# Input projection of an encoder layer: four 512-column chunks taken in two pairs of 1024 columns

## The chip, the cores and the metric

The kernel runs on one core of a Trainium2 chip. The metric is device time in microseconds (us) of one execution; of several executions the median is taken. The core has five engines with queues of their own, which run in parallel and wait for each other through semaphores: PE (TensorE, the matrix engine; PEld is its weight load), DVE (VectorE), ACT (ScalarE), POOL (GpSimd) and SP (SyncE, which here only issues DMAs). An instruction that waits holds up everything behind it in its engine's queue. Matrix products go to PSUM, 8 banks of 512 float32 columns on 128 partitions; all other on-chip data is in SBUF.

## The reference, cut to what matters

One encoder layer on 1024 positions of width 1024. The change touches the input projection and what directly uses its columns.

```python
D_MODEL = 1024; SEQ = 1024; HEAD_DIM = 64; N_HEADS_A = 8; N_KV_A = 2; N_HEADS_B = 8; D_FF = 2816
# w_in: (1024, 2304) -> [qA 512 | kA 128 | vA 128 | qB 512 | kB 512 | vB 512]
hn = rms_norm(x, norm1_g)
proj = hn @ w_in
qa = apply_axial_rope(rms_norm(qa, qa_norm_g), tables)
ka = apply_axial_rope(rms_norm(ka, ka_norm_g), tables)
out_a = global_gqa_attention(qa, ka, va)
out_b = dilated_mixture_attention(rms_norm(qb, qb_norm_g), rms_norm(kb, kb_norm_g), vb)
mixed = jnp.concatenate([rms_norm(out_a, outa_norm_g), rms_norm(out_b, outb_norm_g)], axis=-1)
x = x + mixed @ w_out
x = x + conv_ffn(rms_norm(x, norm2_g), w_up, conv_w, conv_b, w_down)
```

## The kernel before

**Arithmetic.** Everything is float32. An operand of a matrix product is split into a high part (`fp32r`, rounded) and a low part (the rest), and a product takes three matmuls: high by high, high by low, low by high. The split costs one ACT copy (the high part, `bigr<-bigf` in the profile) and one DVE subtraction (the low part, `bigr<-bigf,bigr`).

**Stages.** Load and transpose-load x; the input projection; mixer A (dense attention), mixer B (dilated attention), output projection, up-projection with convolution and gate, down-projection. The input projection has two parts. 256 columns (kA and vA) are done plainly, by `kv_proj(i)` for eight tiles of 128 positions, 24 matmuls of 128x256 each. The other 2048 columns are four chunks of 512, in the order kb, vb, qa, qb, and each chunk is one 2x2 Strassen step: seven products (numbers 1 to 7) of a 512x512 sum of x blocks (`a_op`) by a 512x256 sum of weight blocks. `in_product(m)` is one such product: four tiles of 128 positions, four slices of 128 of the inner dimension, three matmuls of 128x256, so 48 matmuls; there are 28 products.

**Around a product.** `w_load` fetches half a chunk of weights (1 MB), `w_scale` multiplies it by the norm gain on ACT (four instructions of 128x512), `w_prep(m)` forms the weight sum of product m on DVE and splits it (three buffers of 1024 high and 1024 low elements). `in_group(m)` says which two PSUM banks take the product, one of three pairs of banks. `in_out(m)` brings the product out: for numbers 1, 5, 2 and 7 an ACT copy of 128x1024, for 6, 3, 4 and 7 DVE sums; number 6 is added to three other sums in SBUF. `x_squares(i)` squares a tile of x in natural layout (for the norm), with the squares written to PSUM banks that nothing else needs there, and then fetches tile i+2 into the same one of two buffers. `kv_out(i)` copies a tile of kA and vA out of its bank (`kv_bank`, banks 2 to 5). `s_split` makes the x sums of products 3, 5, 6 and 7. `done` makes of a finished chunk what attention needs: squares, norm, rotary turn (on POOL), table products, or a DMA to DRAM. The K heads of mixer A go through `k_fetch`, `k_norm`, `k_turn` (POOL), `k_add`, `k_split` and `k_ready`, spread over products 11 to 27. What remains for qa and qb at the end of the phase is put in a list `late`, from which the attention stages take pieces.

**What sets the order.** All operations are recorded in the order of the Python code, and a list scheduler (`Recorder.simulate`) places them: it prices each operation, follows the dependences, keeps PE nearly in program order and lets other engines take what is ready by their priorities. The result is a fixed order of instructions on each engine. A change in one place therefore can reorder others. Every operation is emitted from one line, L442 before (L444 after), so the groups of a profile are told apart by engine, operands (`bigr` the split operands, `bigf` other SBUF data, `ps` PSUM) and shape.

Of the kernel before, what the change touches and what calls it, by code (L numbers as in the profile page):

```python
# [39 lines left out]
NF = O_F + 9232  # L40
# [20 lines left out]
F_UA = O_F + 1024  # L61
F_WA = (O_F + 2048, O_F + 4096)
F_WC = O_F + 6144
F_NAT = (O_F, O_F + 4096)
F_KVT = O_F + 5120
F_KSQ = O_F + 4096
F_ROPE = O_F + 8192
# [378 lines left out]
def tile_encoder_layer(ctx, tc, x, xt, w_kv, w_in, gains, outg, norm2_g, w_out, w_up, conv,  # L446
# [104 lines left out]
    chunks = ["kb", "vb", "qa", "qb"]  # L551
    prods = [(c, n) for c in range(4) for n in ((1, 5, 2, 7, 6, 3, 4) if c else (1, 2, 5, 7, 6, 3, 4))]
# [44 lines left out]
    def kv_bank(tt):  # L597
        return 2 + tt % 4
# [85 lines left out]
    def w_buf(c, half):  # L684
        return F_WC if half else F_WA[c % 2]

    def w_load(c, half):
        dma(f(w_buf(c, half), 2048), w_in[c, half])

    def w_scale(c, half):  # L690
        for k in range(4):
            o, g = f(w_buf(c, half) + 512 * k, 512), f(SM_G1 + 4 * half + k, 1)
            act(o, o, AF.Copy, scale=g)

    def w_op(m):
        return R_WR + 2048 * (m % 3)

    def w_prep(m):
        if m >= len(prods):
            return  # L700
        c, n = prods[m]
        b11, b12, b21, b22 = [fp(w_buf(c, half) + 256 * u, [512, 4], [1, 256]) for half in range(2) for u in range(2)]
        eng = vec
# [18 lines left out]

    def in_product(m):
        c, n = prods[m]
        w = w_op(m)
        for t in range(4):
            a = a_op(n, t)
            o = PS[:, in_group(m) + 256 * t:in_group(m) + 256 * t + 256]
            for k in range(4):
# [4 lines left out]
                mm(o, al, wh, start=False, stop=(k == 3), skip_group_check=True)

    def c_at(c, t0, u):

        return qab(t0 if c else 4 - t0) + 512 * (c % 2) + 256 * u

    def in_out(m):  # L740
        c, n = prods[m]
# [4 lines left out]
        if n == 1:
            act(ua, g, AF.Copy)
        elif n == 5:
            act(c12, g, AF.Copy)
        elif n == 2:  # L750
            act(c11, g, AF.Copy)
            if c:
                fin(0, 0)
        elif n == 7:
            act(c21, g, AF.Copy)
            add(vec, c22, g, c12)
        elif n == 6:
            add(vec, ua, g, ua)
            for o, eng in ((c22, vec), (c12, vec if c else gp), (c21, vec if c else gp)):
                if c == 3:  # L760

                    last_sums.append(lambda o=o: add(vec, o, o, ua))
                else:
                    add(eng, o, o, ua)
            if c == 0:
                fin(0, 0)
            fin(4, 1)
        elif n == 3:
            add(vec, c12, g, c12)
# [4 lines left out]

    later, deferred, going, n_done, last_sums = [], [], [], [0], []

    def done(c, t0, u, late=None):
# [4 lines left out]

        def v_out():
            for t in range(t0, t0 + 4):
                v = f(o + 1024 * (t - t0), 256)
                act(v, v, AF.Copy, scale=f(SM_R1 + t, 1))
                dma(rows(vscr, t), heads(v, 4))
# [996 lines left out]
```

## Time and profile before

| what | value |
|---|---|
| time, three runs | 1284.65, 1285.03 and 1285.33 us, median 1285.03 |
| the profiled execution, its own time | 1285.81 us |
| its span, first to last instruction | 1284.0 us |
| granted TensorE clock | 1.000 of full speed |
| DVE busy | 1084.5 us, 84% of the span |
| ACT busy | 741.0 us, 58% |
| POOL busy | 112.0 us, 9% |
| DMA moved | 156.99 MB, mean 122 GB/s |

The profiled execution's own time is 1.8 us longer than its span; that stretch lies around the first and last instruction. Busy times of a pipelined PE run from the start of one matmul to its modelled end, so neighbours overlap; rates are therefore read from counts in a window or from the length of an unbroken piece of the chain, not from the mean duration of one matmul. Windows of the span are given in us from the first instruction. The input projection lies between about 10 and 205 us.

### The profile page before, as it was taken

To read this page: it belongs to the slowest core of one execution; us is meant where nothing else is said; L and a number is where in the kernel's file an instruction comes from. 1 tells how busy PE (TensorE), PEld (TensorE's weight loads), DVE (VectorE), ACT (ScalarE), POOL (GpSimd) and SP (SyncE) were. 2 spreads that over 40 slices of the span, in tenths; PEclk is the share of its full clock that TensorE was granted. 3 is DMA by queue.
4 is the path that set the end of the run, shared out by engine and by line. 5 is a ranking of instruction groups with operands and counts; after the bars stand their busy time and mean duration, and the time that the engine had idled before them with its cause. 6 is when DMAs were issued, how large, how long until landed. Compare 5 with 4: busy or idle time off the path is not lost.

```text
span 1284.0 us, 19129 instructions
## 1 busy us (share of the span) xinstructions
PE 1269.3 (99%) x6916; PEld 1080.9 (84%) x6916; DVE 1084.5 (84%) x1906; ACT 741.0 (58%) x1192; POOL 112.0 (9%) x117
## 2 busy tenths in 40 slices
PE   7999999999999999999999999999999999999998
PEld 7999998878888888878888888888888888878887
DVE  6987789999988877897689999999999998776664
ACT  7865467998888776763455444444444444343331
POOL 0011053200212222000120000000000000000000
PEclk9999999999999999999999999999999999999999
DMA  8534211000004554343222322333322347977863
GB/s 334 178 74 116 83 39 55 10 9 1 1 9 113 131 143 101 109 158 131 74 89 68 123 91 75 115 107 107 123 92 83 106 160 259 314 260 234 284 220 113
DMA packets 118206, 156.99 MB, mean 122 GB/s; under 512 B 50656, under 2 KB 75744, under 8 KB 117088
## 3 DMA queue, kind: packets, MB, share of 16 engines
q1 hardware_dynamic: 116816, 152.36, 37.0%
q0 software_dynamic: 1152, 3.15, 0.9%
q8 instruction: 54, 0.88, 0.3%
q10 hardware_dynamic: 144, 0.27, 0.1%
q14 instruction: 40, 0.33, 0.1%
HBM read 117.73 MB, written 33.82 MB: 118 GB/s over the span
## 4 chain that ended last, share of the span: by engine, by line
PE 89%; DVE 4%; DMA 4%; ACT 1%; issue 1%; SPq 0%; ACTq 0%; DVEq 0%
PE ps L442 89%; DVE bigr L442 2%; DVE bigf L442 2%; DMA bigf<-rscr 1%; ACT bigr L442 1%; DMA bigf<-gscr 1%; DMA gscr<-bigf 0%; DMA bigf<-w_down 0%; DMA bigf<-w_out 0%; DMA bigf<-w_kv 0%; ACT L442 0%; SPq L442 0%; ACT bigf L442 0%; ACT ps L442 0%; ACTq L442 0%
## 5 line engine op out<-in xcount | busy, mean ns | idle before, releaser
L442 PE MATMUL ps<-bigr 128*128 128x512 f32 (+3 forms) x6532 | 1238.5, 349 | 9.1 <-ACT bigr L442 6.5
L442 PEld LDWEIGHTS ps<-bigr 128*128 128x128 f32 x6532 | 1042.7, 187 | 183.5 <-ACT bigr L442 13.2
L442 ACT ACTIVATE bigr<-bigf 128x512 fp32r<-128x512 f32 (+2 forms) x358 | 270.6, 770 | 302.4 <-PE ps L442 224.4
L442 DVE TENSOR_TENSOR bigr<-bigf,bigr 128x512 fp32r<-128x512 f32 (+2 forms) x326 | 280.7, 872 | 50.6 <-ACT bigr L442 46.8
L442 DVE TENSOR_TENSOR bigf<-bigf 128x512 f32<-128x512 f32 (+3 forms) x298 | 215.3, 746 | 29.4 <-DMA bigf<-w_down 22.4
L442 DVE TENSOR_TENSOR bigf<-ps,bigf 128x512 f32<-128x512 f32 (+3 forms) x262 | 177.8, 686 | 50.6 <-PE ps L442 43.2
L442 ACT ACTIVATE bigr<-ps 128x512 fp32r<-128x512 f32 (+1 forms) x292 | 167.7, 603 | 85.5 <-PE ps L442 83.3
L442 ACT ACTIVATE bigf<-bigf 128x1024 f32<-128x1024 f32 (+5 forms) x186 | 142.7, 794 | 65.8 <-DVE bigf L442 52.5
L442 DVE SCALAR_TENSOR_TENSOR bigf<-bigf 128x255 f32<-128x255 f32 (+5 forms) x283 | 162.5, 590 | 8.4 <-ACT bigf L442 4.9
L442 DVE TENSOR_TENSOR bigr<-ps,bigr 128x512 fp32r<-128x512 f32 x188 | 127.0, 684 | 29.6 <-ACT ps L442 20.5
L442 ACT ACTIVATE ps<-ps 128x512 f32<-128x512 f32 x192 | 115.3, 602 | 9.4 <-PE ps L442 8.5
L442 ACT ACTIVATE bigf<-ps 128x512 f32<-128x512 f32 (+3 forms) x112 | 71.2, 638 | 56.9 <-PE ps L442 39.7
L442 DVE TENSOR_REDUCE bigf<-ps 128x1 f32<-128x512 f32 x128 | 81.7, 680 | 1.9 <-PE ps L442 1.8
L442 POOL TENSOR_TENSOR bigf<-bigf 128x128 f32<-128x128 f32 (+3 forms) x54 | 56.5, 1071 | 236.3 <-DVE bigf L442 235.9
L442 POOL TENSOR_TENSOR bigr<-bigf,bigr 128x512 fp32r<-128x512 f32 x32 | 42.8, 1341 | 269.7 <-ACT bigr L442 189.3
L442 PE MATMUL ps<-bigf 128*128 128x128 f32 (+2 forms) x384 | 63.0, 294 | 1.4 <-DVE bigf L442 1.3
L442 PEld LDWEIGHTS ps<-bigf 128*128 128x128 f32 (+2 forms) x384 | 43.3, 140 | 15.1 <-DVE bigf L442 2.5
L442 DVE CUSTOM_DVE_ANT_1 bigf<-ps,bigf 128x432 bf16<-128x432 f32 x64 | 38.5, 602 | 2.9 <-PE ps L442 1.9
L442 DVE CUSTOM_DVE_ANT_0 bigf<-ps,bigf 128x256 bf16<-128x256 f32 x64 | 26.9, 420 | 2.5 <-PE ps L442 2.2
L442 DVE TENSOR_REDUCE bigf<-bigf 128x16 f32<-128x1024 f32 x13 | 15.8, 1213 | 2.0 <-ACT bigf L442 2.0
L442 ACT ACT_TABLE_LOAD x11 | 14.1, 1283 | 1.5 <-PEq L1776 1.2
L442 POOL MEMSET bigr<- 64x512 f32 (+2 forms) x18 | 8.2, 479 | 39.0 <-PE ps L442 38.8
(19 smaller groups left out, 60.0 us busy)
## 6 DMA issues: line engine op xcount, KB each, us to landing
bigf<-w_down SPq DMA_DIRECT2D x99, 256.0 KB, 4.0
bigf<-w_up SPq DMA_DIRECT2D x44, 512.0 KB, 3.6
bigf<-gscr SPq DMA_DIRECT2D x77, 256.0 KB, 3.9
gscr<-bigf SPq DMA_DIRECT2D x33, 512.0 KB, 3.7
bigf<-w_in SPq DMA_DIRECT2D x8, 1024.0 KB, 5.7
bigf<-x SPq DMA_DIRECT2D x16, 512.0 KB, 4.7
bigf<-tmx SPq DMA_DIRECT2D x8, 672.0 KB, 4.2
bigr<-bigr SPq DMA_DIRECT2D x16, 256.0 KB, 3.2
```

The costliest lines, as they stand in the source:

```text
L442: method(*args, **kw)
```

## The change

The four chunks become two pairs, (kb, qa) and (qb, vb), of 1024 columns. A product is now a 512x512 sum of x blocks by a 512x512 sum of weight blocks: 48 matmuls of 128x512, one bank for each tile of 128 positions, and there are 14 products. They are issued as 56 quarters (`in_quarter(q)`), each one slice of 128 of the inner dimension for all four tiles, 12 matmuls; `w_prep(q)` makes the weights of one quarter (512 elements, six buffers). The product order is 1, 2, 6, 7, 5, 4, 3 for both pairs. The sums that Strassen adds up are now accumulated in PSUM: `in_group` gives banks 0 to 3 or banks 4 to 7, numbers 1, 6, 5 and 3 run on one group, 2, 7 and 4 on the other, and a product that continues a sum doesn't start a new accumulation. `in_out` then has two copies or two DVE sums of 128x1024 for a product, one for each chunk of the pair, and the SBUF sums of number 6 are gone.

To make room: the x squares are written over their own input, `kv_bank` is banks 4 to 7, the two buffers of natural x lie where the first sums go later, and 3128 columns are added to the SBUF area. Four weight blocks of 1 MB are held per pair, and all four of the first pair are fetched ahead of the first natural x tile. `k_turn` moves from POOL to DVE, the turn of qa is done for four tiles in one instruction, and the rotary table is multiplied by the gain once. What attention needs is prepared during products 12 and 13, on the banks that the other group leaves. Of the deferred work only qb's remains in `late`. The homes of qa and qb in SBUF interleave (`q_at`). The DMA scratch area is set to 2048.

The diff, cut to its core (constants of the SBUF layout, the addresses that follow from `q_at`, the host's layout of w_in and the parts of `done` that only change an address are left out):

```diff
-    chunks = ["kb", "vb", "qa", "qb"]
-    prods = [(c, n) for c in range(4) for n in ((1, 5, 2, 7, 6, 3, 4) if c else (1, 2, 5, 7, 6, 3, 4))]
+    pairs = (("kb", "qa"), ("qb", "vb"))
+    prods = [(p, n) for p in range(2) for n in (1, 2, 6, 7, 5, 4, 3)]
...
     def x_squares(tt):
-        act(PS[:, 3072:4096], f(F_NAT[tt % 2], 1024), AF.Square, accum_out=f(SM_SS1 + tt, 1))
+        act(f(F_NAT[tt % 2], 1024), f(F_NAT[tt % 2], 1024), AF.Square, accum_out=f(SM_SS1 + tt, 1))
...
     def kv_bank(tt):
-        return 2 + tt % 4
+        return 4 + tt % 4
...
     def k_turn():
         for ax in range(2):
             for half in range(2):
-                gp.tensor_tensor(fp(F_KSQ + 32 * ax + 16 * half, [128, 8], [64, 2], [1, 16]),
...
+                o = 32 * ax + 16 * half
+                vec.tensor_tensor(fp(F_KSQ + o, [128, 8], [64, 2], [1, 16]),
+                                  fp(F_TMP + 32 * ax + 16 * (1 - half), [128, 8], [64, 2], [1, 16]),
+                                  fp(F_ROPE + 64 + o, [128, 8], [0, 2], [1, 16]), op=OP.mult)
...
-    def w_prep(m):
+    def w_op(q):
+        return R_WR + 1024 * (q % 6)
+    def w_prep(q):
+        m, k = divmod(q, 4)
         if m >= len(prods):
...
+        p, n = prods[m]
+        b11, b21, b12, b22 = [f(w_block(p, b) + 512 * k, 512) for b in range(4)]
+        if n == 6:
+            vec.tensor_tensor(b12, b22, b12, op=OP.subtract)
+            vec.tensor_tensor(b11, b12, b11, op=OP.add)
+        elif n == 5:
+            vec.tensor_tensor(b12, b22, b11, op=OP.subtract)
         elif n == 4:
-            eng.tensor_tensor(b11, b21, b11, op=OP.subtract)
-        src = {2: b21, 3: b22, 7: b12}.get(n, b11)
-        o = w_op(m)
-        h = rp(o, [256, 4], [1, 256])
-        act(h, src, AF.Copy)
-        vec.tensor_tensor(rp(o + 1024, [256, 4], [1, 256]), src, rfp(o, [256, 4], [1, 256]), op=OP.subtract)
+            vec.tensor_tensor(b11, b21, b11, op=OP.subtract)
+        src = {2: b21, 3: b22, 7: b12, 5: b12}.get(n, b11)
+        o = w_op(q)
+        act(r(o, 512), src, AF.Copy)
+        vec.tensor_tensor(r(o + 512, 512), src, rf(o, 512), op=OP.subtract)
...
     def in_group(m):
-        c, n = prods[m]
-        g = {1: 0, 2: 0, 3: 0, 5: 1, 6: 1, 7: 2, 4: 2}[n]
-        return (0, 1024, 3072)[g if g == 2 else (g + c) % 2]
-    def in_product(m):
-        c, n = prods[m]
-        w = w_op(m)
+        p, n = prods[m]
+        return 4 * ((n in (2, 7, 4)) != p)
+    def in_quarter(q):
+        m, k = divmod(q, 4)
+        n = prods[m][1]
+        w = w_op(q)
+        wh, wl = r(w, 512), r(w + 512, 512)
         for t in range(4):
-            a = a_op(n, t)
-            o = PS[:, in_group(m) + 256 * t:in_group(m) + 256 * t + 256]
-            for k in range(4):
-                ah, al = r(a + 128 * k, 128), r(a + 512 + 128 * k, 128)
-                wh, wl = r(w + 256 * k, 256), r(w + 1024 + 256 * k, 256)
-                mm(o, ah, wh, start=(k == 0 and t % 2 == 0 and n != 2), stop=False, skip_group_check=True)
-                mm(o, ah, wl, start=False, stop=False, skip_group_check=True)
-                mm(o, al, wh, start=False, stop=(k == 3), skip_group_check=True)
-    def c_at(c, t0, u):
-        return qab(t0 if c else 4 - t0) + 512 * (c % 2) + 256 * u
+            a = a_op(n, t) + 128 * k
+            o = bank(in_group(m) + t)
+            mm(o, r(a, 128), wh, start=(k == 0 and (n in (1, 2, 7) or m == 13)), stop=False, skip_group_check=True)
+            mm(o, r(a, 128), wl, start=False, stop=False, skip_group_check=True)
+            mm(o, r(a + 512, 128), wh, start=False, stop=(k == 3), skip_group_check=True)
...
     def in_out(m):
-        c, n = prods[m]
...
+        p, n = prods[m]
+        add = lambda o, i0, i1: vec.tensor_tensor(o, i0, i1, op=OP.add)
+        for i, kind in enumerate(pairs[p]):
+            g, ua = pp(512 * in_group(m) + 256 * i, [512, 4], [1, 256]), fp(F_UA + 1024 * i, [256, 4], [1, 256])
+            c11, c12, c21, c22 = [home(kind, t, u, [1, 256]) for t in (0, 4) for u in range(2)]
+            fin = lambda t0, u: later.append((kind, t0, u))
+            if n == 1:
+                act(ua, g, AF.Copy)
+            elif n == 2:
+                add(c11, g, ua)
                 fin(0, 0)
-        elif n == 7:
-            act(c21, g, AF.Copy)
-            add(vec, c22, g, c12)
-        elif n == 6:
-            add(vec, ua, g, ua)
-            for o, eng in ((c22, vec), (c12, vec if c else gp), (c21, vec if c else gp)):
-                if c == 3:
-                    last_sums.append(lambda o=o: add(vec, o, o, ua))
-                else:
...
-    later, deferred, going, n_done, last_sums = [], [], [], [0], []
...
+            elif n == 6:
+                act(c21, g, AF.Copy)
+            elif n == 7:
+                act(c22, g, AF.Copy)
+            elif n == 5:
+                add(c22, g, c22)
+                fin(4, 1)
+                if p:
+                    act(c12, g, AF.Copy)
+            elif n == 4:
+                add(c21, g, c21)
+                fin(4, 0)
+            elif p:
+                add(c12, g, c12)
+                fin(0, 1)
+            else:
+                act(c12, g, AF.Copy)
+                fin(0, 1)
...
     w_load(0, 1)
     for i in range(6, 8):
         dma(f(qab(i), 1024), xt[i])
+    w_load(0, 2)
+    w_load(0, 3)
     for i in range(2):
         x_nat(i)
...
+    def first_part(i):
+        kv_proj(i)
+        x_sums(i)
+        if i < 7:
+            for half in range(2):
+                x_prep(i + 1, half)
+        s_split(6, i - 4)
+        kv_out(i)
...
+    for i in range(4):
+        when(0, i, lambda i=i: first_part(4 + i))
+        when(0, i, *[lambda j=j: x_squares(j) for j in (2 * i, 2 * i + 1)])
+    when(0, 0, lambda: w_scale(0, 2), lambda: w_scale(0, 3))
+    when(0, 3, late_consts)
+    for m, n in ((1, 7), (2, 5), (3, 3)):
+        for k in range(4):
+            when(m, k, lambda n=n, k=k: s_split(n, k))
...
+    when(10, 2, k_norm, k_turn)
+    when(10, 3, k_add)
+    when(11, 0, k_split)
+    when(12, 0, lambda: bank_rings(range(4, 8)), fill_k, lambda: k_ready(0), lambda: take(prep, 2))
+    when(12, 1, lambda: k_ready(1), lambda: k_ready(2), v_fetch, v_scale)
+    when(12, 2, lambda: k_ready(3), lambda: act(f(SM_T + 96, 1), rf(R_K2A + 512, 1), AF.Exp, scale=0.0))
+    when(12, 3, lambda: v_ops(0), lambda: v_ops(4), lambda: take(prep, 1))
+    when(13, 0, lambda: bank_rings(range(4)))
+    for k in range(1, 4):
+        when(13, k, lambda: take(prep, 2))
+    for q in range(56):
+        in_quarter(q)
+        m, k = divmod(q, 4)
+        if k == 3:
+            finished()
+        for fn in at.get((m, k), ()):
+            fn()
+        if k == 3:
+            in_out(m)
+        w_prep(q + 6)
     take(prep, 99)
...
-    late = last_sums + [t for d in deferred[:2] for t in done(*d, 0)[3:]]
...
+    finished()
+    late = []
+    parts = [done(*d, i) for i, d in enumerate(deferred)]
     late += [t for p in parts for t in p[0]] + [t for p in parts for t in p[1]]
```

Three places in the order show what moved. First PE, from the first matmul on, without the waits. The 128x256 matmuls are `kv_proj` and, before the change, the products. Before, the kv tiles and the first 23 products read as one row, and the 128x128 rows are K transposes between the products that follow:

```order
L442 MATMUL ps<-bigr 128x256 x1296
L442 MATMUL ps<-bigr 128x128 x4
L442 MATMUL ps<-bigr 128x256 x48
L442 MATMUL ps<-bigr 128x128 x4
L442 MATMUL ps<-bigr 128x256 x48
L442 MATMUL ps<-bigr 128x128 x4
L442 MATMUL ps<-bigr 128x256 x48
L442 MATMUL ps<-bigr 128x128 x8
```

After, the 128x512 rows are the products; 12 of them are one quarter:

```order
L444 MATMUL ps<-bigr 128x256 x96
L444 MATMUL ps<-bigr 128x512 x12
L444 MATMUL ps<-bigr 128x256 x24
L444 MATMUL ps<-bigr 128x512 x12
L444 MATMUL ps<-bigr 128x256 x24
L444 MATMUL ps<-bigr 128x512 x12
L444 MATMUL ps<-bigr 128x256 x24
L444 MATMUL ps<-bigr 128x512 x12
L444 MATMUL ps<-bigr 128x256 x24
L444 MATMUL ps<-bigr 128x512 x544
L444 MATMUL ps<-bigr 128x128 x8
L444 MATMUL ps<-bigr 128x512 x8
```

The last four kv tiles now each follow a quarter of the first product, and the K transposes stand among the quarters of product 12, which is the 13th.

Second ACT, at the end of the first product. Before, the row `bigf_63<-ps_65 128x1024` is the copy of the first product out of PSUM; it comes ahead of the weight scaling (`bigf_63<-bigf_63 128x512`) and of the squares of tiles 2 to 7, of which the last row here (`ps_65,bigf_63<-bigf_63`) is the first:

```order
L442 ACTIVATE bigr_64<-bigf_63 128x512
L442 ACTIVATE bigr_64<-bigf_63 128x512 [waits DMAHW6_49]
L442 ACTIVATE bigr_64<-bigf_63 128x512
L442 ACTIVATE bigf_63<-ps_65 128x1024 [waits PE_49]
L442 ACTIVATE bigr_64<-bigf_63 128x1024 [waits DVE_49]
L442 ACTIVATE bigr_64<-bigf_63 128x512 [waits DVE_49] x2
L442 ACTIVATE bigf_63<-bigf_63 128x512 [waits DMAHW3_49]
L442 ACTIVATE bigf_63<-bigf_63 128x512 x3
L442 ACTIVATE bigr_64<-bigf_63 128x1024 [waits Activation_49]
L442 ACTIVATE ps_65,bigf_63<-bigf_63 128x1024 [waits DMAHW6_49]
```

After, `bigf_63<-bigf_63 128x1024` with a wait for a DMA is a square of a natural x tile, and `bigf_63<-ps_65 128x1024` are the two copies of the first product:

```order
L444 ACTIVATE bigf_63<-bigf_63 128x512
L444 ACTIVATE bigf_63<-bigf_63 128x1024 [waits DMAHW6_49]
L444 ACTIVATE bigr_64<-bigf_63 128x512 [waits DVE_49,PE_49]
L444 ACTIVATE bigr_64<-bigf_63 128x512
L444 ACTIVATE bigf_63<-bigf_63 128x1024 [waits DMAHW7_49]
L444 ACTIVATE bigr_64<-bigf_63 128x512 [waits DVE_49,PE_49]
L444 ACTIVATE bigr_64<-bigf_63 128x512 x2
L444 ACTIVATE bigf_63<-bigf_63 128x1024 [waits DMAHW2_49]
L444 ACTIVATE bigf_63<-ps_65 128x1024 [waits Activation_49]
L444 ACTIVATE bigf_63<-bigf_63 128x1024 [waits DMAHW3_49]
L444 ACTIVATE bigf_63<-ps_65 128x1024 [waits Activation_49]
L444 ACTIVATE bigr_64<-bigf_63 128x512 [waits PE_49]
```

The first copy now stands behind the square of tile 6, the second behind that of tile 7, the last.

Third DVE, at the K heads of mixer A. Before, the rows from `TENSOR_REDUCE` on are `k_norm` (a reduction, small root steps, two products), two low parts of weights, and `k_add`, whose first sum waits for the turn on POOL:

```order
L442 TENSOR_REDUCE bigf<-bigf 128x16
L442 SCALAR_TENSOR_TENSOR bigf<-bigf 128x16 [waits DVE_49]
L442 RECIPROCAL bigf<-bigf 128x16 [waits Activation_49]
L442 TENSOR_TENSOR bigf<-bigf 128x16 [waits DVE_49]
L442 SCALAR_TENSOR_TENSOR bigf<-bigf 128x16 [waits DVE_49] x2
L442 TENSOR_TENSOR bigf<-bigf 128x1024 [waits DMAHW5_49,DVE_49]
L442 TENSOR_TENSOR bigf<-bigf 128x1024 [waits DVE_49]
L442 TENSOR_TENSOR bigr<-bigf,bigr 128x1024 [waits PE_49,Activation_49]
L442 TENSOR_TENSOR bigr<-bigf,bigr 128x1024 [waits Activation_49]
L442 TENSOR_TENSOR bigf<-bigf 128x1024 [waits DVE_49,Pool_49]
L442 TENSOR_TENSOR bigf<-bigf 128x1024 [waits DVE_49]
```

After, the rows are the two products of `k_norm`, the four instructions of `k_turn`, the two sums of `k_add`, the low part of the weights of the first quarter of product 12, a weight sum, the two sums of product 11 out of PSUM, and `k_split`:

```order
L444 TENSOR_TENSOR bigf<-bigf 128x1024 [waits DMAHW1_49,DVE_49]
L444 TENSOR_TENSOR bigf<-bigf 128x1024 [waits DVE_49]
L444 TENSOR_TENSOR bigf<-bigf 128x16x16 [waits DMAHW0_49,DVE_49]
L444 TENSOR_TENSOR bigf<-bigf 128x16x16 x3
L444 TENSOR_TENSOR bigf<-bigf 128x1024 [waits DVE_49] x2
L444 TENSOR_TENSOR bigr<-bigf,bigr 128x512 [waits PE_49]
L444 TENSOR_TENSOR bigf<-bigf 128x512
L444 TENSOR_TENSOR bigf<-ps,bigf 128x4x256 [waits DMAHW3_49,DMAHW2_49,DMAHW7_49,PE_49,Activation_49]
L444 TENSOR_TENSOR bigf<-ps,bigf 128x1024
L444 TENSOR_TENSOR bigr<-bigf,bigr 128x16x64 [waits Activation_49]
```

The turn is now in DVE's queue, and the low part of the weights for product 12 stands behind it.

More of the change, by code (lines that the diff above doesn't have):

```diff
@@ L39 @@
 O_F = O_QAB + 8192
-NF = O_F + 9232
+NF = O_F + 12360
 R_XT = 0
@@ L60 @@
 F_TMP = O_F
[L61 to L67, printed above, removed]
+F_W = [O_F + 1024 + 2048 * i for i in range(4)]
+F_KVT = O_F
+F_KST = O_F + 12296
+F_KSQ = F_W[1]
+F_UA = O_F + 10248
+F_WC = F_UA
+F_NAT = (F_UA, F_UA + 1024)
+F_VS = O_F + 4096
+F_ROPE = O_F + 9216
 R_QD = R_XT
@@ L781, in done @@
+    later, n_done = [], [0]
+    def done(kind, t0, u, late=None):
         rows = lambda dst, t: dst[4 * u:4 * u + 4, 128 * t:128 * t + 128, :].rearrange("h p d -> p h d")
+        whole = home(kind, t0, u, [64, 4], [1, 64])
+        tile = lambda i: whole[:, i]
         def v_out():
[L784 to L787, printed above, removed]
+            for i in range(4):
+                act(tile(i), tile(i), AF.Copy, scale=f(SM_R1 + t0 + i, 1))
+                dma(rows(vscr, t0 + i), tile(i))
@@ L816, in norm, with turn @@
         def norm():
[L817 to L824 removed]
+            vec.tensor_tensor(whole, whole, fp(t, [4, 4], [1, 4], [0, 64]), op=OP.mult)
+        def turn(ax, half):
+            o = 32 * ax + 16 * half
+            gp.tensor_tensor(fp(so + o, [256, 4], [64, 4], [1, 16]),
+                             fp(q_at(1, t0, u) + 32 * ax + 16 - 16 * half, [1024, 4], [64, 4], [1, 16]),
+                             fp(F_ROPE + 128 * t0 + 64 + o, [128, 4], [0, 4], [1, 16]), op=OP.mult)
         def cos():
[L827 removed]
+            vec.tensor_tensor(whole, whole, fp(F_ROPE + 128 * t0, [128, 4], [0, 4], [1, 64]), op=OP.mult)
         def add():
[L830 removed]
+            vec.tensor_tensor(whole, whole, sq, op=OP.add)
         def gain():
[L833 removed]
+            gp.tensor_tensor(whole, whole, fp(O_GB, [0, 4], [0, 4], [1, 64]), op=OP.mult)
         def k_out():
             for i in range(4):
[L837 removed]
+                dma(rows(kscr, t0 + i), tile(i))
         if kind == "qa":
[L840 removed]
+            return [square, root, norm] + [lambda a=a, b=b: turn(a, b) for a in range(2) for b in range(2)] + [cos, add]
         if kind == "kb":
@@ new lines, in first_part, with finished, when @@
+    def first_part(i):
[6 more added lines that the diff above has]
+        kv_out(i)
+    def finished():
+        ready, later[:] = later[:], []
+        for d in ready:
+            if d[0] == "qb":
+                deferred.append(d)
+            else:
+                for t in done(*d):
+                    t()
+    deferred = []
+    at = {}
+    def when(m, k, *fns):
+        at.setdefault((m, k), []).extend(fns)
@@ new lines, in tile_encoder_layer, with rstd @@
+    for i in range(4):
+        when(0, i, lambda i=i: first_part(4 + i))
[5 more added lines that the diff above has]
+            when(m, k, lambda n=n, k=k: s_split(n, k))
+    def rstd():
+        vec.tensor_scalar(v, f(SM_SS1, 8), 1.0 / D, EPS, op0=OP.mult, op1=OP.add)
+        act(rt, v, AF.Sqrt)
+        newton(f(SM_R1, 8), v, rt, f(SM_SS1, 8))
```

210 lines of the change are left out of this document (47 added, 163 removed).

## The prediction

> **What bounds the kernel now.** I read the page's busy row and its chain first, then PE's waits in the stretch that the change touches (0 to 220 us), then windows of 20 us inside it.
>
> ```profile
> PE 1269.3 (99%) x6916; PEld 1080.9 (84%) x6916; DVE 1084.5 (84%) x1906; ACT 741.0 (58%) x1192; POOL 112.0 (9%) x117
> ...
> PE 89%; DVE 4%; DMA 4%; ACT 1%; issue 1%; SPq 0%; ACTq 0%; DVEq 0%
> ...
> PE ps L442 <- ACT bigr L442: 6.5, 2, 6.4
> PE ps L442 <- DVE bigr L442: 0.8, 2, 0.6
> ...
> 36.08 148.29 PE ps L442 x1238
> ```
>
> PE is busy for 99% of the span and carries 89% of the chain. Up to 220 us it waits 6.4 us once, for the first operands, and hardly again: in the chain the products are one piece from 36.08 on, 1238 matmuls in 148.29 us, 119.8 ns each. So the pace of PE sets this stage.
>
> ```profile
> core 0: us, PE busy (x) PEld busy (x) DVE busy (x) ACT busy (x) POOL busy (x), PEclk, DMA share, GB/s
> 0.00:20.00 20.00, 13.30 (x91) 12.71 (x92) 10.54 (x22) 12.68 (x22) 0.21 (x4) 1.00 0.92 350
> 20.00:40.00 20.00, 19.43 (x162) 19.23 (x161) 18.75 (x26) 18.26 (x33) 0.00 (x0) 1.00 0.68 246
> 40.00:60.00 20.00, 20.00 (x169) 20.00 (x168) 18.49 (x27) 17.00 (x27) 0.00 (x0) 1.00 0.41 139
> 60.00:80.00 20.00, 20.00 (x169) 20.00 (x169) 15.78 (x27) 13.69 (x20) 5.77 (x2) 1.00 0.25 100
> 140.00:160.00 20.00, 20.00 (x169) 20.00 (x168) 16.84 (x18) 6.83 (x10) 1.82 (x5) 1.00 0.14 28
> 180.00:200.00 20.00, 19.82 (x157) 18.93 (x157) 18.73 (x30) 8.05 (x15) 9.71 (x16) 1.00 0.29 86
> 200.00:220.00 20.00, 19.91 (x92) 15.19 (x92) 19.27 (x32) 17.07 (x34) 7.52 (x10) 1.00 0.11 29
> 300.00:400.00 100.00, 99.89 (x520) 81.13 (x520) 91.06 (x188) 87.06 (x163) 13.52 (x7) 1.00 0.07 15
> ```
>
> From 60 to 160 us DVE and ACT have slack. Towards both ends, 20 to 60 and 180 to 220, DVE is nearly full, and so is ACT in 20 to 60: there the change can lose what it wins.
>
> **The pace of PE.** The products' 28x48 = 1344 matmuls of 256 columns become 672 of 512. The up-projection shows 512-column matmuls with split operands, unbroken:
>
> ```profile
> 1131.98 145.84 PE ps L442 x642
> ```
>
> 145.84/642 = 227.2 ns. So two small ones cost 239.6 and a large one 227.2, 12.4 less. A matmul thus shows a fixed part: if 256 columns more cost 107.4, then 12.4 is left of each. Over 672 pairs that is 8.3 us. Start-to-start times inside these pieces are 120.0 and 226.7 ns, which gives 13.3 ns a pair and 672x13.3 = **8.9 us less**; I take 8.9, since the pieces hold a few shorter transposes and an open end.
>
> The Trainium skill, "TensorE: Matmul & The Clock Gate", section "Back-to-back issue gap", speaks against that: N/2.4 + 2.5 ns for a warm matmul, so about 109 and 216 ns, a pair would save 2.5 ns and the whole 1.7 us. The rows above disagree with it, 119.8 and 227.2 ns in this kernel.
>
> **The head: first sums behind the squares of x.** Product 6 is third and accumulates on the banks of product 1's sum. It may begin only when both ACT copies of that sum (one for each chunk) are done, and by the order they now stand in ACT's queue behind the squares of tiles 6 and 7. Before, the copy stood ahead of the squares of tiles 2 to 7, and nothing that PE needed soon stood behind those squares' loads.
>
> ```profile
> 6.36 3.63 PE L442 MATMUL ps<-bigr 128*128 128x256 f32 x13 [6.36 <-ACT bigr L442]
> 10.24 10.03 PE L442 MATMUL ps<-bigr 128*128 128x256 f32 x78 [0.25 <-DVE bigr L442]
> ...
> 15.43 2.55 ACT L442 ACTIVATE bigf<-bigf 128x512 f32<-128x512 f32 x4
> ...
> 21.06 1.01 ACT L442 ACTIVATE ps<-bigf 128x1024 f32<-128x1024 f32 x1
> ...
> 26.91 1.03 ACT L442 ACTIVATE bigf<-ps 128x1024 f32<-128x1024 f32 x1 [1.18 <-PE ps L442]
> ...
> 33.38 1.01 ACT L442 ACTIVATE ps<-bigf 128x1024 f32<-128x1024 f32 x1
> ...
> 34.54 1.03 ACT L442 ACTIVATE ps<-bigf 128x1024 f32<-128x1024 f32 x1
> 35.51 0.19 ACT L442 ACTIVATION_READ_ACCUMULATOR ps<-bigf 128x1 f32 x1
> 35.60 0.64 ACT L442 ACTIVATE bigf<-ps 128x256 f32<-128x256 f32 x2
> ...
> 40.90 1.03 ACT L442 ACTIVATE ps<-bigf 128x1024 f32<-128x1024 f32 x1 [1.37 <-DMA bigf<-x]
> 41.87 0.19 ACT L442 ACTIVATION_READ_ACCUMULATOR ps<-bigf 128x1 f32 x1
> ...
> 46.30 1.03 ACT L442 ACTIVATE ps<-bigf 128x1024 f32<-128x1024 f32 x1 [0.66 <-DMA bigf<-x]
> 47.26 0.18 ACT L442 ACTIVATION_READ_ACCUMULATOR ps<-bigf 128x1 f32 x1
> 47.35 3.22 ACT L442 ACTIVATE bigr<-bigf 128x512 fp32r<-128x512 f32 x6
> ...
> bigf<-x SPq DMA_DIRECT2D x16, 512.0 KB, 4.7
> ```
>
> When PE would be there: 91 matmuls have begun by 20.2 us; 101 of the kv tiles remain (x 0.120 = 12.1) and 96 of products 1 and 2 (x 0.2267 = 21.8), so 54.1 us. When ACT is: its first rows up to the weight scaling at 15.43 are the same in both. Ahead of the first square now stand 14 scalings (0.64 each by 2.55/4), 18 splits (0.52 by 3.22/6, less the overlap) and a kv copy (0.34), 18.7 us. One split takes a weight buffer that quarter 2 of the first product frees at 34.8 us, by the same PE count, some 1.7 us after ACT is there. So square 0 starts at about 15.4 + 18.7 + 1.7 = 35.8. From there squares 2, 4 and 6 chain: a load goes out only when the square two tiles earlier has read its buffer. A step is 1.16 (33.38 to 34.54) plus the load: 5.2 us in one case (the square at 34.54 ends at 35.7, its successor starts at 40.90), 4.2 in another (41.87 + 0.19 to 46.30), 4.7 on the page. Three steps of 5.9 give 53.5 for the start of square 6; then square, copy (0.95), square 7, copy: 57.7. **PE loses 3.6 us** (0.7 of it already at product 2, whose third bank is a kv bank that ACT empties late). With loads of 4.2 it is 2.1, of 5.2 it is 5.1; if no square waited, ACT's own work (37.4 us from 15.43, and 1.7) would leave 0.5. Before, this stretch lost 0.6 (19.43 busy from 20 to 40). Net +3.0.
>
> The Trainium skill, "DMA: Bandwidth & Descriptors", section "Anatomy of one DMA — SWDGE (gpsimd) path", gives 2.0 us plus bytes over 436 GB/s, an estimate of 3.2 us for 512 KB. The squares would then hardly wait and the net be about 0; the trace's 4.2 to 5.2 us contradict it on SP's queue.
>
> **The tail: K heads in DVE's queue.** From product 10's end ACT and DVE do in order: a copy of the sum, a small root, a weight split, the square of K, its reduction, a norm, four small steps, two products, now the four turns, two sums, and only then the low part of the weights of product 12.
>
> ```profile
> L442 ACT ACTIVATE bigr<-bigf 128x512 fp32r<-128x512 f32 x236 | 144.9, 628 | 149.4 <-PE ps L442 110.1 <-DVE bigf L442 24.2 <-issue 12.8
> L442 DVE TENSOR_TENSOR bigr<-bigf,bigr 128x512 fp32r<-128x512 f32 x196 | 135.0, 702 | 9.2 <-ACT bigr L442 7.4 <-PE ps L442 0.8
> L442 ACT ACTIVATE bigf<-bigf 128x1024 f32<-128x1024 f32 x87 | 99.8, 1148 | 51.6 <-DVE bigf L442 41.2 <-DMA gscr<-bigf 9.1 <-issue 1.1
> L442 DVE TENSOR_TENSOR bigf<-bigf 128x1024 f32<-128x1024 f32 x68 | 82.3, 1223 | 3.4 <-POOL bigf L442 2.9
> L442 DVE TENSOR_TENSOR bigf<-ps,bigf 128x256 f32<-128x256 f32 x32 | 13.5, 422 | 1.4
> L442 DVE SCALAR_TENSOR_TENSOR bigf<-bigf 128x16 f32<-128x16 f32 x31 | 4.8, 163 | 0.4
> ...
> 201.44 0.02 issue
> 201.46 0.69 DVE bigf L442
> 202.15 0.61 DVE bigr L442
> 202.76 0.04 issue
> ```
>
> That is ACT 1.0 + 0.2 + 0.6 + 1.1, then DVE six of 1.2 (the reduction and five of 1024), five small ones 0.8, four turns 1.7 (0.42 each, by the nearest shape), a low part 0.7: 13.3 us, or 12.2 with the overlap of back-to-back rows. PE arrives after 48 + 4 matmuls, 11.8 us: late by 0.4 to 1.5, I take 1.0. Behind it DVE has a weight sum, product 11's two sums and `k_split`, 4.3 us, and the K transposes come 12 matmuls (2.7 us) later: another 1.6. With 0.4 at the start of attention, 3.0. Before, its end lost between 0.3 (what PE lacks of busy in 180 to 220) and 1.4 or more (the chain's DVE pieces at 201.44); nearest to the chain, with the 0.3, I take 1.7. **Net +1.3**; the ends are -1.7 (the new tail fits) and +3.
>
> **At nothing.** 56 weight splits of 512 for 28 of 1024 add some 5 us each to ACT and DVE; twelve 1.2 us sums leave DVE. Both lie under PE from 60 to 160 us, where DVE has 3 and ACT 6 of 20 us free; without that cover it would be 5. Two more blocks of 1 MB ahead of x take 6 us at 350 GB/s; the first square began at 21.06, so x lands by about 27, and is needed at 35.8. Later weight loads have whole products of time. The attention stages get 13 late pieces instead of 30, on DVE and POOL; PE lacks 0.1 us there from 300 to 400, so at most 1 us either way.
>
> **Sum.** -8.9 + 3.0 + 1.3 = -4.6: 1285.8 - 4.6 = 1281.2 by the profiled execution's own time, which is 0.8 above the median of the runs; by the median 1280.4. I say **1280.6**.
>
> **The rivals.** *Nothing is lost* at either end (short loads, K chain in time): for it, the long gap-free piece and DVE's dropped sums; against it, the squares that waited 1.37 and 0.66 us. -8.9 + 0 - 0.3, about 1276. *The ends eat it*: loads of 5.2 (net +4.5) and the late K chain at +3: -1.4, about 1283.6, within 0.2% (2.6 us, about what a measurement of this kernel can tell from no change). *Every product boundary waits*: sums now stay in two groups of four banks, and each of 13 boundaries may find its group still being read by ACT or DVE, two instructions of about 1 us that sit in order among the weight splits. From 0.7 us a boundary the gain is gone, from 0.9 it is slower by over 0.2%; a whole pair of copies, 1.9 us, would give 1285 - 8.9 + 25 = 1301; I put it at 1289. Against it: a group rests one product, 10.9 us, between uses, and ACT has slack. *The change doesn't do what it says*: the fixed part of a matmul doesn't halve, and the gain is 1.7 instead of 8.9, with the same stalls: 1287.6. Against it stand the two rates. This is the case that the page of the Trainium skill on TensorE implies.
>
> **How the numbers follow.** Forecast (1278.5 to 1282.5) 0.48, nothing lost 0.22, eaten 0.18, boundaries 0.09, no halving 0.03. The range takes the first three: 1275.5 to 1285. Faster by over 0.2%: forecast nearly whole and nothing lost, 0.70; within 0.2%: eaten and the rest of the forecast, 0.19; slower 0.11.
>
> **What would show it.** After the change: products at 227 ns in the chain; PE idle of about 3 us for `ACT bigf` near 54 us and squares waiting for `DMA bigf<-x` ahead of it; PE waiting for `DVE bigr` near 165 us, 1 to 3 us. Wrong if PE waits at many boundaries between 60 and 150 us, if the matmuls run slower than 227 ns, or if the squares don't wait.

## The result, and the profile after

| kernel | median, us | runs | lowest and highest |
|---|---|---|---|
| before | 1285.37 | 6 | 1284.65 to 1285.93 |
| after | 1318.70 | 6 | 1316.41 to 1322.20 |

The ratio is 1.0262, with a 95% interval of 1.0248 to 1.0276: the change made the kernel slower by 2.6%, where 1280.6 us were forecast. The profiled execution of after has a span of 1316.7 us against 1284.0, so 32.7 us have to be found.

First the page of after: the rows of PE and DVE with busy time, share of the span and instructions, and the chain's shares by engine.

```profile
PE 1272.9 (97%) x6244; PEld 1050.3 (80%) x6244; DVE 1082.1 (82%) x1946; ACT 747.1 (57%) x1220; POOL 86.1 (7%) x88
PE 80%; DVE 6%; DMA 6%; issue 3%; ACT 3%; POOL 1%; SPq 1%; ACTq 0%; DVEq 0%; POOLq 0%
```

PE had 89% of the chain and now has 80%. No engine's busy time grew by more than 6.1 us, so most of the time is in waits. Next, PE's own waits in after between 30 and 300 us (engine, operand, what it waited for: us in total, times, longest).

```profile
PE ps L444 <- DVE bigr L444: 6.4, 4, 4.3
PE ps L444 <- ACT bigf L444: 3.4, 2, 2.9
PE ps L444 <- ACT bigr L444: 0.3, 1, 0.3
```

Most of this is the two stalls of the forecast: the ACT copy at the head (0.5 and 2.9), and DVE at the tail (4.3 and 0.2; the other two waits of that row, 1.0 each, lie in the attention, at 280 and 294 us). All together they come to 10 us and the faster matmuls give 8.9 back, so they can't make 32.7. The rest shows only far behind the changed stage, in windows of the down-projection of after:

```profile
core 0: us, PE busy (x) PEld busy (x) DVE busy (x) ACT busy (x) POOL busy (x), PEclk, DMA share, GB/s
1085.00:1105.00 20.00, 20.00 (x90) 16.57 (x89) 10.41 (x13) 5.00 (x5) 0.00 (x0) 1.00 0.60 199
1105.00:1120.00 15.00, 13.03 (x55) 9.79 (x54) 9.96 (x12) 4.02 (x4) 0.00 (x0) 1.00 0.55 178
1120.00:1140.00 20.00, 15.58 (x54) 11.29 (x53) 11.81 (x15) 4.77 (x5) 0.00 (x0) 0.83 0.61 204
1140.00:1160.00 20.00, 7.86 (x27) 5.53 (x25) 9.11 (x11) 3.49 (x4) 0.00 (x0) 0.82 0.87 307
1160.00:1180.00 20.00, 17.34 (x69) 14.19 (x70) 9.55 (x11) 7.10 (x7) 0.00 (x0) 0.84 0.43 132
```

A window of 20 us at full pace holds 90 matmuls; these hold 54, 27 and 69. No engine is full there, nor is DMA (0.87 at most). Before, PE was busy for all but 0.8 us of the same stretch (the row below is 1100 to 1165 of before):

```profile
1100.00:1165.00 65.00, 64.17 (x283) 52.46 (x281) 49.50 (x59) 24.21 (x24) 0.00 (x0) 1.00 0.78 262
```

No line of the diff touches the down-projection, and the order of the instructions on every engine in the last 700 us is that of before. What waits there? The waits of after between 1085 and 1200, and under them those of before that answer to them:

```profile
ACT bigr L444 <- DMA bigf<-w_down: 31.6, 6, 7.3
ACT bigr L444 <- DMA bigf<-gscr: 27.9, 9, 8.0
PE ps L444 <- DVE bigf L444: 10.7, 1, 10.7
PE ps L444 <- ACT bigr L444: 5.9, 3, 3.4
```

```profile
ACT bigr L442 <- PE ps L442: 44.2, 25, 4.4
ACT bigr L442 <- DMA bigf<-gscr: 17.5, 6, 4.6
PE ps L442 <- DVE bigf L442: 0.8, 2, 0.6
```

Before, ACT mostly waited for PE to free an operand: it was ahead. After, it waits for loads of `w_down` and `gscr`: it is behind. The chain of after in that stretch (start us, us, what) shows how:

```profile
1085.82 3.19 DMA bigf<-gscr
...
1089.18 4.77 DMA bigf<-w_down
1094.13 1.07 ACT bigr L444
1095.23 1.24 DVE bigr L444
1096.48 2.63 DMA bigf<-gscr
1099.22 1.07 ACT bigr L444
1100.31 2.52 DMA bigf<-w_down
1102.94 1.24 DVE bigr L444
1104.20 2.69 DMA bigf<-gscr
1107.12 1.07 ACT bigr L444
```

Load, split on ACT, low part on DVE, next load: the steps run one after the other. There are four buffers for these loads, which should let them run ahead; here a split waits for a load that goes out only when an earlier step is done with its buffer, although that load isn't the one it reads.

The instructions are the same, but what they are built to wait for isn't. Below are three of ACT's instructions from the built program of after (number, line, operation, operands, shape). Each name in the brackets is a semaphore, `DMAHW` those of transfers:

```
1058 L444 ACTIVATE bigr<-bigf 128x1024 [waits DMAHW0_49,DMAHW6_49,DVE_49,DMAHW7_49,PE_49,Activation_49]
1060 L444 ACTIVATE bigr<-bigf 128x1024 [waits DMAHW4_49,DMAHW6_49,DVE_49,PE_49]
1062 L444 ACTIVATE bigr<-bigf 128x1024 [waits DMAHW4_49,DMAHW3_49,DMAHW5_49,DMAHW1_49,DMAHW7_49,DVE_49,PE_49]
```

and the same three in the changed kernel with its SBUF area 8 columns wider:

```
1058 L444 ACTIVATE bigr<-bigf 128x1024 [waits DMAHW6_49,PE_49,Activation_49]
1060 L444 ACTIVATE bigr<-bigf 128x1024 [waits DVE_49,DMAHW5_49,PE_49,Activation_49]
1062 L444 ACTIVATE bigr<-bigf 128x1024 [waits DVE_49,DMAHW5_49,PE_49,Activation_49]
```

One transfer each there; up to five here, and up to eight among the 22 splits of this kind. The rows belong to `d_prep`, in products 5 and 6 of the down-projection. There the source of a split is one operand of two pieces far apart:

```python
F_DR = F_UR = [O_F + 5632, O_F + 6656, O_F + 7680, O_F + 2560]      # four buffers of loads
...
o, d, t = F_DR[m % 4], R_D[m % 6], F_T[q]
src = fp(t, [o + 512 - t, 2], [1, 512]) if n in (5, 6) else fp(o, [512, 2], [1, 512])
act(rp(d, [512, 2], [1, 512]), src, AF.Copy)
```

The change widened the SBUF area from 18256 columns (16 x 1141) to 21384, which is not a multiple of 16. Of the four widths in the kernels shown here, the multiples of 16 (18256 and 21392) have the short lists, and the other two (18264 and 21384) the long ones. That made the first theory. The lists look as if the build took such an operand for all that lies between its pieces; why a multiple of 16 keeps it from that stays open.

### The profile page after: what moved, and what is told of

Its sections match the earlier page's. It is cut to its first block, busy times and chain, and to the rows that moved or that the text cites. A ratio compares the mean times of both kernels' runs of the same rounds, so it can differ in the third digit from the quotient of the medians.

```text
span 1316.7 us, 17822 instructions
## 1 busy us (share of the span) xinstructions
PE 1272.9 (97%) x6244; PEld 1050.3 (80%) x6244; DVE 1082.1 (82%) x1946; ACT 747.1 (57%) x1220; POOL 86.1 (7%) x88
## 4 chain that ended last, share of the span: by engine, by line
PE 80%; DVE 6%; DMA 6%; issue 3%; ACT 3%; POOL 1%; SPq 1%; ACTq 0%; DVEq 0%; POOLq 0%
PE ps L444 80%; DVE bigf L444 4%; DVE bigr L444 2%; DMA bigf<-w_down 2%; ACT bigr L444 1%; DMA bigf<-gscr 1%; POOL bigf L444 1%; DMA gscr<-bigf 1%; DMA bigf<-x 1%; ACT bigf L444 1%; SPq L444 1%; DMA bigf<-kvscr 0%; DMA kvscr<-bigf 0%; DMA bigf<-w_kv 0%; DMA bigf<-rscr 0%
## 5 line engine op out<-in xcount | busy, mean ns | idle before, releaser
L444 PEld LDWEIGHTS ps<-bigr 128*128 128x128 f32 x5860 | 1012.4, 187 | 246.7 <-DVE bigr L444 22.8
L444 ACT ACTIVATE bigr<-bigf 128x512 fp32r<-128x512 f32 (+2 forms) x386 | 275.2, 729 | 339.3 <-PE ps L444 192.2
L444 DVE TENSOR_TENSOR bigf<-bigf 128x512 f32<-128x512 f32 (+5 forms) x312 | 212.0, 702 | 36.2 <-DMA bigf<-w_down 15.4
L444 DVE TENSOR_TENSOR bigf<-ps,bigf 128x512 f32<-128x512 f32 (+3 forms) x260 | 174.7, 682 | 50.5 <-PE ps L444 36.8
L444 ACT ACTIVATE bigf<-bigf 128x1024 f32<-128x1024 f32 (+5 forms) x194 | 152.8, 806 | 66.9 <-DVE bigf L444 49.4
L444 POOL TENSOR_TENSOR bigf<-bigf 128x256 f32<-128x256 f32 (+2 forms) x25 | 30.8, 1251 | 207.4 <-DVE bigf L444 89.0
```

Of the source, the lines that this page charges most:

```text
L444: method(*args, **kw)
```

## The experiments

The theories at the start. **A:** at a width that is no multiple of 16 the build adds waits that the data don't need, in stages that the change doesn't touch; that is the loss of about 30 us, and without it the kernel is near the forecast. **B:** the loss is in something else that the change brings along, the wider area, the smaller DMA scratch area, or accesses that are slower at that width.

A measure used below is the delay of a matmul: the last 5300 matmuls do the same work in all kernels, but for a few in the same order, so counted from the end they can be paired, and their start compared with the profiled execution of before. In us, at the place where before stands at the time of the heading:

| kernel | 210 | 271 | 293 | 373 | 1097 | 1135 | 1280 |
|---|---|---|---|---|---|---|---|
| after | 0.5 | 2.4 | 4.7 | 4.9 | 4.8 | 33.1 | 33.2 |
| e_pad | -0.1 | 1.7 | 0.4 | 0.6 | 0.2 | -1.2 | -1.2 |
| b_8 | 9.2 | 9.2 | 10.0 | 13.7 | 13.7 | 45.8 | 45.8 |
| b_pad | -0.4 | -0.5 | -0.5 | -0.5 | -0.4 | -1.9 | -1.9 |
| e_split | 1.9 | 3.8 | 6.2 | 6.4 | 6.1 | 4.6 | 4.6 |
| c_tail | -4.7 | -4.1 | -5.4 | -5.2 | -5.7 | -7.1 | -7.1 |
| c_head | -2.3 | -0.4 | -1.7 | -1.5 | -1.7 | -3.2 | -3.2 |
| c_both | -9.0 | -8.4 | -9.7 | -9.4 | -9.8 | -11.2 | -11.2 |

(The profile of before itself lost about 1.4 us between 1097 and 1135, which the others gain there.)

**e_pad: the changed kernel, 8 columns wider.**

```diff
-NF = O_F + 12360
+NF = O_F + 12368
```

> The changed kernel with 8 more columns of SBUF (12368 for 12360), nothing else: the row of the area is then 21392 columns, a multiple of 16 (64 bytes), as it was before (18256), and in the order the additional waits of the down-projection's weight splits for neighbouring loads are gone. Theory A (those waits hold ACT and DVE up between 1085 and 1165 us and cost the 28 us there): 1288 to 1294 us, no PE idle of more than 2 us between 1080 and 1180. Rival B (the loads are late because the whole kernel arrives some 4 us later and with one more DMA, so the lanes are shifted): 1315 to 1320. Rival C (PE's clock, granted at 0.82 to 0.84 there, starts it): also 1315 to 1320.

Measured: 1285.71 us (1283.61 to 1289.74, 10 runs), ratio to before 1.0008 (0.9999 to 1.0018). Eight columns that nothing uses took 33 us away, more than the text above gave to theory A. Its rivals B (shifted loads) and C (the clock as the start of it) left the time at 1315 us or more, and fall. Windows of e_pad:

```profile
40.00:60.00 20.00, 16.72 (x81) 13.59 (x80) 15.86 (x32) 16.55 (x31) 2.35 (x1) 0.96 0.54 161
60.00:80.00 20.00, 20.00 (x87) 16.43 (x86) 16.16 (x31) 12.06 (x19) 0.00 (x0) 0.96 0.26 82
80.00:160.00 80.00, 80.00 (x355) 66.26 (x354) 65.14 (x110) 45.75 (x73) 17.32 (x26) 1.00 0.26 72
160.00:180.00 20.00, 15.41 (x74) 12.21 (x73) 18.27 (x29) 12.59 (x21) 1.92 (x4) 1.00 0.22 49
1100.00:1165.00 65.00, 65.00 (x288) 53.85 (x287) 49.55 (x58) 25.04 (x25) 0.00 (x0) 1.00 0.79 264
```

The down-projection is whole again, and the ends of the input projection keep their stalls (16.72 and 15.41 of 20 busy). It also says what is left to explain: without the width the change is worth nothing, where -4.6 us were forecast.

**b_8: the kernel before, 8 columns wider, and nothing else.**

```diff
-NF = O_F + 9232
+NF = O_F + 9240
```

> The kernel before with 8 more columns of SBUF (9240 for 9232), nothing else: a row of 18264 columns is no multiple of 16, and the same additional waits appear in its down-projection. Theory A: slower, 1300 to 1315 us, with PE idle between 1100 and 1160 us. Rivals B and C: 1285 us, as before, since neither the projection nor the number of DMAs changes.

Measured: 1332.77 us (1331.73 to 1336.58, 4 runs), ratio 1.0374 (1.0358 to 1.0390), more than either theory said. The kernel before has none of the change here, and shows the same signature in its waits between 1085 and 1200:

```profile
ACT bigr L442 <- DMA bigf<-w_down: 31.2, 6, 7.2
PE ps L442 <- DVE bigf L442: 10.3, 1, 10.3
```

By the table it loses 32 us in the down-projection, and 9.2 and 3.7 more before 210 and between 293 and 373, where its own two-piece operands weren't followed up.

**b_pad: the kernel before with the wide area and the small scratch area, at a multiple of 16.**

```diff
-NF = O_F + 9232
+NF = O_F + 12368
...
-    nc = _bacc.Bacc("TRN2", target_bir_lowering=False, num_devices=1)
+    nc = _bacc.Bacc("TRN2", target_bir_lowering=False, num_devices=1, dynamic_dma_scratch_size=2048)
```

> The kernel before, with nothing of the change but the SBUF area widened to O_F + 12368 (21392 columns, a multiple of 16; 3136 more than it needs) and the DMA scratch area of 2048 that makes the room. Theory A (only the width's remainder by 16 matters, neither its size nor the scratch area): same as before, 1284 to 1286.5 us. Rival C (the wider area or the smaller scratch costs time of itself, so that a part of what the 8 columns more gave back is something else): 1288 us or more.

Measured: 1284.82 us (1284.00 to 1285.87, 11 runs), ratio 1.0001 (0.9992 to 1.0010). Neither the size of the area nor the scratch area costs anything.

**e_split: the width of the change kept, the two-piece splits of products 5 and 6 divided.** This tells the waits from slower accesses, since all addresses and the row's length stay as in after.

```diff
+        if n in (5, 6):
+            for i, src in enumerate((t, o + 512)):
+                act(r(d + 512 * i, 512), f(src, 512), AF.Copy)
+                vec.tensor_tensor(r(d + 1024 + 512 * i, 512), f(src, 512), rf(d + 512 * i, 512), op=OP.subtract)
+            return
         src = fp(t, [o + 512 - t, 2], [1, 512]) if n in (5, 6) else fp(o, [512, 2], [1, 512])
```

> The changed kernel with its own width of the SBUF area (21384 columns, not a multiple of 16), but the splits of the down-projection's products 5 and 6, whose source is one instruction over two pieces far apart, divided into two instructions of 512 columns each, on ACT and on DVE. Theory A (at this width the build reads such a two-piece source as everything between its pieces, and so waits for loads that it doesn't need): the idle PE between 1100 and 1165 us goes, granted clock 1.0 there, time 1286 to 1291 us, as with 8 columns more (1285.7), plus little for 22 more instructions on ACT and on DVE. Rival B (the width itself slows accesses and transfers to SBUF): the loss stays, 1312 to 1320 us.

Measured: 1289.64 us (1286.16 to 1292.98, 10 runs), ratio 1.0036 (1.0026 to 1.0046). Windows of e_split:

```profile
1120.00:1140.00 20.00, 20.00 (x90) 16.58 (x89) 17.07 (x28) 8.78 (x16) 0.00 (x0) 1.00 1.03 374
1140.00:1160.00 20.00, 20.00 (x89) 16.55 (x89) 12.83 (x18) 8.29 (x12) 0.00 (x0) 1.00 0.57 176
```

With 22 instructions more on ACT and on DVE the stretch runs at full pace: the loss there came from the waits of these instructions alone. Rival B falls. The profile's pages agree: a `w_down` load takes 3.7 us in after and in e_pad alike. That e_split stays 4 us above e_pad comes to over half from the start of attention: between 271 and 293 after and e_split lose 2.3 and 2.4 us against before, and e_pad gains 1.3. Between 270 and 300 after has this row, twice 1.8 us, and e_pad none like it:

```profile
ACT bigr L444 <- POOL bigf L444: 3.6, 2, 1.8
```

In the built program the two splits, which begin at 278.34 and 292.25 us in after, have POOL in their lists at the width of after, and empty lists in e_pad. They read 256 columns that lie between the four pieces that POOL's instruction writes. So it looks like the same fault with an operand of four pieces; no run shows it alone.

**Now the two ends.** What e_pad still loses has two candidates, each with an edit of its own. At the tail its chain shows why the K heads come late:

```profile
149.24 3.13 POOL bigf L444 x4
...
152.40 1.24 DVE bigf L444
...
154.95 5.97 DMA bigf<-kvscr
...
161.02 1.07 ACT bigf L444
...
171.90 0.68 DVE bigr L444
172.58 2.87 DVE bigf L444 x3
175.45 1.14 DVE bigr L444
...
176.64 23.92 PE ps L444 x120
```

The K heads are fetched (`bigf<-kvscr`) into the buffer `F_TMP`, which the squares and turns of kb and qa use too. So the fetch waits for qa's turns on POOL and the sum behind them, takes 6 us, and only then comes the square of K at 161.02.

**c_tail: e_pad, with the K heads in a place of their own** (that of product 1's sums, free from product 9 on), and fetched there.

```diff
-        dma(heads(f(F_TMP, 1024), 8), kvscr[:, :, 0:128].rearrange("t p c -> p t c"))
+        dma(heads(f(F_UA, 1024), 8), kvscr[:, :, 0:128].rearrange("t p c -> p t c"))
...
-    when(8, 0, k_fetch, lambda: dma(f(F_ROPE, 1024), rope))
+    when(8, 0, lambda: dma(f(F_ROPE, 1024), rope))
+    when(9, 0, k_fetch)
```

> The changed kernel with 8 columns more, and the K heads of mixer A fetched at product 9 into the place of product 1's sums, so that they no longer wait for the turns of qa, which write the same buffer before. Theory A (the gaps of 3.8 us near 168.6 and 1.1 us near 175 are the K heads' chain, which starts late because of that buffer): both gaps go, 1281 to 1283 us against 1285.7 with the 8 columns alone. Rival B (DVE and ACT are simply too busy in products 10 to 12, and the weights of product 12 would be late without the chain too): gaps of 3 us or more stay in 160 to 180, 1284.5 to 1286.5 us.

Measured: 1279.57 us (1278.28 to 1280.75, 5 runs), ratio 0.9958 (0.9946 to 0.9971), 1.4 us below the range said. Its window from 160 is whole:

```profile
160.00:180.00 20.00, 20.00 (x99) 16.38 (x98) 18.68 (x27) 13.20 (x22) 2.34 (x6) 1.00 0.35 74
```

**c_head: e_pad, with three buffers of natural x.** The third is the rotary table's place; the table is loaded behind the last tile that uses it.

```diff
-F_NAT = (F_UA, F_UA + 1024)
+F_NAT = (F_UA, F_UA + 1024, F_ROPE)
...
-        if tt < 6:
-            x_nat(tt + 2)
+        if tt < 5:
+            x_nat(tt + 3)
+        if tt == 5:
+            dma(f(F_ROPE, 1024), rope)
...
-    for i in range(2):
+    for i in range(3):
         x_nat(i)
-    dma(f(F_ROPE, 1024), rope)
```

> The changed kernel with 8 columns more, and three buffers of natural x instead of two (the third is the rotary table's place, which is loaded later). Theory A (the 2.9 us of idle PE near 54 us are the chain of loads and squares of x, two tiles at a time): the square of the last tile comes before product 1's end, the gap falls under 1 us, and what the clock loses after it (1.7 us) falls with it: 1281.5 to 1284 us. Rival B (ACT is late for reasons of its own, with the copies behind other work): gap of 2 us or more stays, 1285 to 1286.5 us.

Measured: 1281.29 us (1279.71 to 1282.26, 7 runs), ratio 0.9971 (0.9960 to 0.9982), at the lower edge of what was said, and in the windows where e_pad has 81 and 87 matmuls:

```profile
40.00:60.00 20.00, 19.25 (x96) 16.07 (x96) 17.06 (x33) 17.51 (x33) 0.00 (x0) 1.00 0.41 129
60.00:80.00 20.00, 20.00 (x90) 16.58 (x89) 18.88 (x37) 15.03 (x23) 2.50 (x1) 1.00 0.47 158
```

The gap of 2.7 us that e_pad has there is gone, one of 0.8 is left.

**c_both: both edits.**

> Both of the two before: K heads in their own buffer and three buffers of natural x, with 8 columns more. If both theories hold and the two are independent: PE idle in the whole input projection from 45 to 195 us under 2 us, 1277 to 1280 us, faster than the kernel before. If the ends share what is lost (later stages take it back): 1281 to 1284 us.

Measured: 1273.80 us (1272.60 to 1274.21, 4 runs), ratio 0.9913 (0.9900 to 0.9927): faster than both kernels, 0.9% under before. PE's only wait between 30 and 300 us, and the piece of the chain through the products:

```profile
PE ps L444 <- DVE bigr L444: 0.2, 1, 0.2
```

```profile
45.42 146.09 PE ps L444 x658
```

The two losses add up to within 1 us. It came out 3 us better than said; the single edits lower e_pad's ratio by 0.0050 and 0.0037, 11 us together, and c_both stands 11.9 us under e_pad.

## Why the prediction was wrong

**The step that failed** is "At nothing", and with it the sum. It ends with "at most 1 us either way" for the attention stages, and has no term for what lies behind them. The SBUF area's new width was in the diff and got no price at all. It costs 33 us (e_pad against after), by the table of delays some 30 of them in the down-projection and 3.6 at the start of attention. No rival covered it either: the slower one, waits at every product boundary, didn't occur: PE has no wait in after between 60 and 150 us. The built program showed it before any run: the order of the down-projection's instructions was the same, but their lists of waits weren't. The step weighed the order alone.

**The pace** held. Between 80 and 160 us matmuls start 226.7 ns apart in e_pad, and those of half the size 120.0 ns apart in before: 13.3 ns less a pair, as was said. (The counts of such a window, 355 and 669, take in matmuls that lie across its edges.) The rule of the Trainium skill ("TensorE: Matmul & The Clock Gate", section "Back-to-back issue gap") by which a pair would save 2.5 ns doesn't hold in this kernel; the page gives it for isolated matmuls, and says that in a stream with weight loads both set the pace.

**The head** was right in place, cause and size, for what was counted: 3.6 us said, 3.4 in after's waits for `ACT bigf`. The figure of the Trainium skill ("DMA: Bandwidth & Descriptors", section "Anatomy of one DMA — SWDGE (gpsimd) path") that the forecast set against these loads is one for DMAs issued from GpSimd; these are issued on SP, so they don't contradict it. What wasn't counted is the clock behind the gap. In e_pad PE stands still for 2.7 us until 57.38, and then:

```profile
58.00:62.00 4.00, 4.00 (x12) 3.14 (x11) 2.98 (x5) 2.44 (x5) 0.00 (x0) 0.57 0.00 0
62.00:66.00 4.00, 4.00 (x19) 3.28 (x19) 3.07 (x5) 3.95 (x8) 0.00 (x0) 1.00 0.00 0
```

The first window holds 12 matmuls at a granted clock of 0.57 where 19 fit, so some 1.6 us more are lost. It happened in e_pad, c_tail and e_split, and not at this place in after, though its gap was as long. The Trainium skill ("TensorE: Matmul & The Clock Gate", section "Part 1: The HAM clock gate (the "warmup" mystery)") describes such a gate, which goes to half rate after an idle window of about 3.4 us that runs freely against the kernel. The half rate agrees with the trace (0.50 in e_pad from 58.4 to 61.5 us), and so does the luck of the moment; the length doesn't, since the gap here was shorter. c_head, which takes the gap away, gives back 0.0037 of the time, 4.8 us, against the 3.0 net that the sum had.

**The tail** was right in place and mis-sized. The working started the K chain "from product 10's end"; it starts later, at the fetch, which shares `F_TMP` with the turns of qa. That is a chain over SP and POOL, and the step read only ACT's and DVE's queues. PE lost 3.6 and 1.0 us there in e_pad instead of 3.0, and c_tail gives back 0.0050, 6.4 us, partly at the start of attention. The net term was +1.3. It had also taken off 1.7 for what before loses at its own tail; in the trace of before PE waits 0.2 us there.

**The sum with measured terms** closes at the end of the projection. By the traces of e_pad and before: -8.9 for the pace, +3.3 for the waits at the head and +1.6 for the clock behind them, +4.6 at the tail, and -0.8 for the waits of before between 30 and 300 us. That is -0.2, where the table of delays has -0.1 at 210 us. Without the two ends it leaves -9.7; c_both has -9.0 there, and -11.2 at the end of the kernel. Of the 2.2 between, 1.4 are what the profile of before lost by itself; the rest stays open.

The rival "nothing is lost" (about 1276) thus comes nearest to the change as it could have been, 1273.8 in c_both. By the working's own terms for before, 0.6 and 1.7, it should have said 1274: its sum took off 0.3. The change as written gave all of its gain back at its ends and 33 us on top through a number of the layout.

## What to carry to other kernels

When a change alters the size of a shared buffer, compare the waits of the built instructions everywhere, not their order alone: here a row length that wasn't a multiple of 16 columns made instructions on two far-apart pieces wait for other buffers' loads, 900 us behind the changed stage. In such a kernel try a multiple of 16 first, or give each piece its own instruction. And for each step of a chain that must be in time, ask which buffer it writes and who still reads it: both stalls at the ends came from a shared buffer, and both went with another place for the data.

## What the runs showed of the hardware

Idle PE can cost more than its idle time. Behind gaps of 2.7 to 2.9 us the granted clock was 0.57 to 0.62 on the mean from 58 to 62 us in e_pad, c_tail and e_split, and 1.00 in after from 58 to 62 us, where the gap was 2.9 us too. Behind the gap at the tail it was 1.00 from 172 to 176 us in e_pad (3.6 us idle), and 0.65 in after (4.3 us). The means hide two values: 0.50 in e_pad from 58.4 to 61.5 us, and 1.00 behind that.

In the broken stretch of after the mean was 0.82 to 0.84 from 1120 to 1180 us, though PE was busy for 41 of those 60 us. From 1105 to 1180 PE was idle for 21 us, and the stretch lost 28 by the table of delays; the other 7 are, as an estimate, what the lower clock cost. Since the clock doesn't fall in every run, this also spreads the times: e_pad's ten runs lie 6.1 us apart, c_both's four, without the gaps, 1.6.
